# Gathering the next position's tokens ahead of the last turning of h in an expert stage

## The chip, the core and the metric

The kernel runs on one core of a Trainium2 chip as a single launch. The time is the device time of that core in microseconds (us), the median of several runs. The profile is one further execution of the same program, recorded by the hardware profiler. TensorE (PE) multiplies matrices, its weight loads are shown as PEld, VectorE is DVE, ScalarE is ACT, GpSimd is POOL, and SyncE (SP) issues the DMAs. Each engine runs its own list of instructions, and semaphores tie the lists together.

## What is computed

A two-layer encoder over 256 tokens of width 1024: a gated convolution and pooling mixer, cross-attention and a dense SwiGLU in the first layer; a Conformer convolution, cross-attention and a mixture of experts in the second; then an RMSNorm. The change is in the mixture of experts:

```python
def moe_swiglu(xn, router, w_gu, w_down):
    logits = (xn @ router).astype(jnp.float32)
    top_v, top_i = lax.top_k(logits, TOP_K)          # 2 of 8 experts for each token
    w = jax.nn.softmax(top_v, axis=-1)
    comb = jnp.sum(jax.nn.one_hot(top_i, N_EXPERTS, dtype=jnp.float32) * w[..., None],
                   axis=-2).astype(xn.dtype)
    out = jnp.zeros_like(xn)
    for e in range(N_EXPERTS):
        out = out + comb[..., e:e + 1] * swiglu(xn, w_gu[e], w_down[e])
    return out
```

with `swiglu(x) = (silu(x @ g) * (x @ u)) @ w_down`, g and u of 1024 x 3584 and w_down of 3584 x 1024 for each of the eight experts, all in float32.

## The kernel before

The experts are processed one after the other in eight "positions". For a position the tokens that chose its expert are gathered into `xg` by a product with a one-hot matrix, go through gate, up and down products, and their result is scattered back by a product with the turned one-hot matrix. Positions 2, 4 and 6 take experts with few tokens (at most 64, `NARROW`), positions 1, 3, 5 and 7 those with up to 128 (`WIDE`). So each narrow position is followed by a wide one.

A float32 operand is used as two parts: a rounded `hi`, made by a cast on ScalarE (L168), and the rest `lo`, made by a subtraction on VectorE (L169). Each weight chunk of 1 MB is loaded by one DMA, 13 chunks ahead, and is split in two halves into four buffers each for `hi` and for `lo`. A wide position multiplies the token parts separately, with three products for a pair. A narrow position lays the hi and lo parts of its 64 tokens side by side in 128 columns of `xg` (L1054, L1055), so that each weight part needs one product; the two halves of the result are added afterwards (`fold`, L1143).

A position has seven steps j. A step of a narrow position (`step_narrow`, L1163) makes the gate product `pg` and the up product `pu` of 512 hidden columns: `xs[:4]`, the first 512 columns of `xg`, in a first pass and `xs[4:]` in a second. The second pass of the up product takes its weights whole, without a split (L1193). In between it turns the h of the step before (L1155, `ht`, against a matrix that also adds the two halves), and it ends with that step's down products into `py`. h itself (`eh`, L1206) comes from the fold, a Silu on ScalarE and a multiplication on VectorE. After the seventh step three things are left: turning h of step 6 (`to_rows`, L1209, with the copy and the subtraction of L1054 and L1055 behind it), gathering the tokens of the following position (`following.rows`, L1069; for a wide one 16 products of 128 x 128 from L1043, `gx`, in two halves, each followed by a copy to the hi part, L1075, and a subtraction to the lo part, L1076, of `xg`), and the last down products. There is one `xg`.

The order on TensorE, VectorE and ScalarE in this stage is set by a scheduler that takes the program and places each instruction as soon as its inputs, its buffers and its engine are expected to be free. `tc.issue_after(i)` holds what is written inside it behind instruction i. Only the order on the queue that issues DMAs is as written.

Of the kernel before, what the change touches and what calls it, by code (L numbers as in the profile page):

```python
# [32 lines left out]
P = 128  # L33
D = 1024
# [41 lines left out]
def build(tc, io, cap=CAP):  # L76
    ctx = ExitStack()
    with ctx:
        _build(ctx, tc, io, cap)


def _build(ctx, tc, io, cap):
# [15 lines left out]
    V, S, G, PE = nc.vector, nc.scalar, nc.gpsimd, nc.tensor  # L98

    def f32(ap):  # L100
        return ap.bitcast(F32)

    def big_tile(name, dt=F32):
        return big.tile([P, CH], dt, tag="big", name=name)
# [7 lines left out]
    def tr_tile(name="tr", dt=F32):  # L112
        return psT.tile([P, 512], dt, tag="tr", name=name)
# [14 lines left out]
    def col(name, i=0):  # L128
        o = _OFF[name] + i
        return vec[:, o:o + 1]  # L130
# [19 lines left out]
    done, casts = [], []  # L150
# [553 lines left out]
    for m in range(KD):  # L704
# [6 lines left out]
        for hf in range(2):  # L711
# [4 lines left out]
            for kk in range(half):  # L716
                k = hf * half + kk
                h, sl = hid[k // 8], slice((k % 8) * T, (k % 8 + 1) * T)
# [22 lines left out]
    for k in range(KD):  # L741
        last = V.scalar_tensor_tensor(a3[:, k * T:(k + 1) * T], hT[:, k, :], col("od_norm_mix", k), rb,
                               op0=ALU.mult, op1=ALU.mult)
# [25 lines left out]
    def conv31(c):  # L769
        def tap(k):  # L770
            return glu[c][:, k:k + T], col("od_dw_w", c * CK + k)
        part = work.tile([P, T], F32, tag=("part", "sqs")[c % 2], name="part")
        src, w = tap(0)
        S.activation(part, src, AF.Identity, bias=col("od_dw_b", c), scale=w)
        taps = G_TAPS[c]
        for k in range(1, taps):
            src, w = tap(k)
            prod = work.tile([P, T], F32, tag="w1", name="prod", bufs=w1b)
            S.activation(prod, src, AF.Copy, scale=w)
            G.tensor_add(part, part, prod)  # L780
        y = tr_tile("cacc")[:, :T]
        src, w = tap(taps)
        V.tensor_scalar_mul(y, src, w)
        for k in range(taps + 1, CK):
            src, w = tap(k)
            V.scalar_tensor_tensor(y, src, w, y, op0=ALU.mult, op1=ALU.add)
        return V.tensor_add(cv[:, c * T:(c + 1) * T], y, part)
# [11 lines left out]
    last = conv31(KD - 1)  # L799
# [47 lines left out]
    for k in range(KD):  # L847
# [5 lines left out]
        last = V.tensor_sub(p2[1][:, sl], x1, f32(p2[0][:, sl]))  # L853
# [33 lines left out]
    xt = big_tile("xt")  # L887
# [149 lines left out]
    def gathered(oh, q):  # L1037

        px = tr_tile("gx")
        for kk in range(4):  # L1040
            d0 = (4 * q + kk) * P
            for t in range(2):
                PE.matmul(px[:, kk * P:(kk + 1) * P], xt[:, t * D + d0:t * D + d0 + P],  # L1043
                          oh[:, t, :], start=t == 0, stop=t == 1)
        return px

    def slots(p):
# [9 lines left out]
    class Gather:  # L1057
# [11 lines left out]
        def rows(self):  # L1069
            if self.e in NARROW:  # L1070
                return self.rows_narrow()
            for q in range(2):
                px = gathered(self.oh, q)
                hi, lo = xg[:, q * 512:(q + 1) * 512], xg[:, D + q * 512:D + (q + 1) * 512]
                S.copy(hi, px)  # L1075
                V.tensor_sub(lo, px, f32(hi))  # L1076

        def rows_narrow(self):
            px = tr_tile("gx")
            for k in range(KD):  # L1080
                for t in range(2):
                    PE.matmul(px[:, k * HALF:(k + 1) * HALF],
                              xt[:, t * D + k * P:t * D + (k + 1) * P],
                              self.oh[:, t, :HALF], start=t == 0, stop=t == 1)
            side_by_side(xg[:, :D], px)
# [42 lines left out]
    def expert(e, g, following):  # L1128
        nonlocal fn
        py = out_tiles()  # L1130
        two = e in NARROW

        def gate_up(j, gu):
            pz = acc_tile("gu")
            for kh in range(2):
                w = chunk()
                ws = [w(kk * 512, (kk + 1) * 512) for kk in range(4)]
                moving(pz, [(xg[:, k * P:(k + 1) * P], xg[:, D + k * P:D + (k + 1) * P])
                            for k in range(kh * 4, kh * 4 + 4)],
                       ws, kh == 0, kh == 1)  # L1140
            return pz
# [9 lines left out]
        def turn_narrow(j, h):  # L1151

            pt = tr_tile("ht")
            for i in range(4):
                ins = PE.matmul(pt[:, i * HALF:(i + 1) * HALF], h[:, i * P:(i + 1) * P], both,  # L1155
                                start=True, stop=True)
            return pt, ins

        def rows_narrow(j, pt):
            o = (j % 2) * D  # L1160
            side_by_side(ht[:, o:o + 512], pt[:, :4 * HALF])

        def step_narrow(j, h):  # L1163

            xs = [xg[:, k * P:(k + 1) * P] for k in range(KD)]
            tiles = [(f * 512, (f + 1) * 512) for f in range(4)]  # L1170

            def parts(w):
                return [w(*sl) for sl in tiles]
            pg, pu = acc_tile("gu"), acc_tile("gu")
            g0 = chunk()
            g1 = chunk()
            last = narrow(pg, xs[:4], parts(g0), True, False)
            u0 = chunk()
            if j:
                with tc.issue_after(last.ins):  # L1180
                    pt, last = turn_narrow(j - 1, h)
                with tc.issue_after(casts[-1].ins):
                    rows_narrow(j - 1, pt)
            with tc.issue_after(last.ins):
                narrow(pg, xs[4:], parts(g1), False, True)
            u1 = whole_chunk()
            d0 = chunk() if j else None
            narrow(pu, xs[:4], parts(u0), True, False)
            d1 = chunk() if j else None
            with tc.issue_after(casts[-2 if j else -1].ins):  # L1190
                sg = fold(pg)
            for kk in range(4):
                last = PE.matmul(pu, f32(xs[4 + kk]), u1[:, kk * 512:(kk + 1) * 512],  # L1193
                                 start=False, stop=kk == 3)
            with tc.issue_after(casts[-1].ins):
                h = gate(sg, pu)
            if j:
                down(j - 1, 0, d0)
                down(j - 1, 1, d1)
            return h  # L1200

        def gate(pg, pu):
            sg = pg if two else work.tile([P, 512], F32, tag="w2", name="esg", bufs=w2b)
            S.activation(sg, pg, AF.Silu, scale=g.cw[:, 1:2])
            h = work.tile([P, 512], F32, tag="w2", name="eh", bufs=w2b)
            V.scalar_tensor_tensor(h, pu, g.cw[:, 1:2], sg, op0=ALU.mult, op1=ALU.mult)  # L1206
            return h

        def to_rows(j, h):  # L1209
            pt = tr_tile("ht")  # L1210
            o = (j % 2) * D
            if two:
                return rows_narrow(j, turn_narrow(j, h)[0])
            for i in range(4):
                PE.transpose(pt[:, i * P:(i + 1) * P], h[:, i * P:(i + 1) * P], ident)
            S.copy(ht[:, o:o + 512], pt)
            V.tensor_sub(ht[:, o + 512:o + D], pt, f32(ht[:, o:o + 512]))
# [29 lines left out]
        h = None  # L1247
        for j in range(7):
            if two:
                h = step_narrow(j, h)  # L1250
                if j == 6:
                    to_rows(6, h)
                if following is not None and j in (3, 5):
                    following.step(j)
                continue
            pg = gate_up(j, 0)
            if j:
                to_rows(j - 1, h)
            pu = gate_up(j, 1)
            h = gate(pg, pu)  # L1260
            if j:
                down(j - 1, 0)
                if j == 6:
                    to_rows(6, h)
                down(j - 1, 1)
            if following is not None and j in (3, 5):
                following.step(j)
        if following is not None:
            following.rows()
        else:  # L1270
            fn = big_tile("fn")
            nc.sync.dma_start(fn[:, :D], io["final_norm"].to_broadcast([P, D]))
        down(6, 0)
        y = weighted(0)
        last = down(6, 1)
# [98 lines left out]
    for e in range(NE):  # L1374
        following = Gather(e + 1) if e + 1 < NE else None
# [7 lines left out]
    def overflow(e):  # L1383
        oh = one_hot(e, slots(e), P, F32)
        xo = big_tile("xo")
        for q in range(2):
            S.copy(xo[:, q * 512:(q + 1) * 512], gathered(oh, q))
# [164 lines left out]
```

## Time and profile before

| what | value |
|---|---|
| median of 3 runs (lowest, highest) | 1527.86 us (1527.21, 1529.25) |
| the profiled execution: its time / its span | 1527.87 us / 1526.1 us |
| TensorE busy | 1499.1 us, 98% of the span |
| VectorE, ScalarE, GpSimd busy | 85%, 69%, 10% |
| mean granted TensorE clock | 0.995 of full speed |
| read from HBM | 448.75 MB, 295 GB/s over the span |
| the expert stage | from about 587 us to about 1510 us |
| ends of positions 2, 4, 6 | about 931, 1157 and 1383 us |

Busy time of TensorE counts matmuls that follow each other through a pipeline, with modelled ends. In a row of the timeline the number in brackets is the time that the engine was idle before it, and behind the arrow what released it. One product of float32 operands shows as two records in the rows of `ht`, `gx` and the whole-weight pass (x8 for four products, x32 for sixteen).

### The profile page before, as it was taken

How to read it: one execution, taken by the hardware profiler on the slowest of the kernel's cores; microseconds unless marked ns; L12 is line 12 of the kernel's file. 1: busy time of each engine (PE TensorE's matmuls, PEld its weight loads, DVE VectorE, ACT ScalarE, POOL GpSimd, SP SyncE). 2: the span in 40 equal slices, each digit the busy share in tenths (PEclk: the TensorE clock that was granted, in tenths of full speed). 3: DMA queues.
4: the chain of work that ended last, by engine and by line, in shares of the span. 5: the costliest groups of instructions: out<-in, count | busy, mean ns of one | idle time of the engine just before them, and what ended most of it. 6: DMA issues, size and time to landing. Idle time of an engine off the chain costs nothing.

```text
span 1526.1 us, 23758 instructions
## 1 busy us (share of the span) xinstructions
PE 1499.1 (98%) x8558; PEld 1298.5 (85%) x8558; DVE 1302.1 (85%) x1735; ACT 1056.3 (69%) x1381; POOL 148.1 (10%) x230
## 2 busy tenths in 40 slices
PE   8999999999999999999999999999999999999996
PEld 8899999999988998888888777888777888777885
DVE  7876677776898867999898999998999998998996
ACT  6554554455576656777777887777887777887775
POOL 4710000001295201000000000000000000000000
PEclk9999999999999999999999999999999999999998
DMA  9754354426644665999999999999999999999940
GB/s 370 278 193 166 138 177 166 140 89 217 228 146 190 214 249 199 372 373 340 356 374 345 383 421 421 391 375 349 380 420 422 404 372 341 394 421 421 388 178 30
DMA packets 65215, 451.44 MB, mean 296 GB/s; under 512 B 7360, under 2 KB 7488, under 8 KB 12480
## 3 DMA queue, kind: packets, MB, share of 16 engines
q1 hardware_dynamic: 65088, 449.83, 76.9%
q8 instruction: 69, 1.13, 0.3%
q14 instruction: 58, 0.48, 0.1%
HBM read 448.75 MB, written 1.05 MB: 295 GB/s over the span
## 4 chain that ended last, share of the span: by engine, by line
PE 88%; POOL 4%; DVE 3%; ACT 2%; issue 1%; DMA 1%; SPq 0%; POOLq 0%; DVEq 0%; ACTq 0%
PE gu L217 8%; PE gu L213 8%; PE gu L212 8%; PE gu L1124 7%; PE acc L206 7%; PE acc L205 7%; PE acc L204 7%; PE py L1124 5%; PE gu L1193 4%; PE py L217 4%; PE py L212 4%; PE py L213 4%; POOL part L780 2%; PE ht L1155 1%; PE gx L1043 1%
## 5 line engine op out<-in xcount | busy, mean ns | idle before, releaser
L169 DVE TENSOR_TENSOR lo<-raw,hi 128x1024 fp32r<-128x1024 f32 (+3 forms) x573 | 673.2, 1209 | 101.1 <-ACT hi L168 81.3
L168 ACT CAST hi<-raw 128x1024 fp32r<-128x1024 f32 (+3 forms) x573 | 569.9, 1031 | 258.4 <-PE acc L205 89.7
L169 DVE TENSOR_TENSOR lo<-spare,hi 128x1024 fp32r<-128x1024 f32 (+1 forms) x226 | 261.7, 1201 | 17.5 <-ACT hi L168 12.1
L168 ACT CAST hi<-spare 128x1024 fp32r<-128x1024 f32 (+1 forms) x226 | 224.0, 1035 | 49.8 <-PE gu L213 27.9
L212 PE MATMUL gu<-hi,xg 128*128 128x512 f32 x560 | 219.5, 392 | 0.0
L213 PE MATMUL gu<-hi,xg 128*128 128x512 f32 x560 | 218.8, 391 | 0.0
L217 PE MATMUL gu<-lo,xg 128*128 128x512 f32 x560 | 157.3, 392 | 0.0
L212 PEld LDWEIGHTS gu<-hi,xg 128*128 128x128 f32 x560 | 105.2, 188 | 22.0 <-ACT hi L168 0.2
L213 PEld LDWEIGHTS gu<-hi,xg 128*128 128x128 f32 x560 | 105.3, 188 | 21.6
L217 PEld LDWEIGHTS gu<-lo,xg 128*128 128x128 f32 x560 | 104.8, 188 | 22.0
L212 PE MATMUL py<-hi,ht 128*128 128x512 f32 x280 | 109.4, 393 | 0.0
L213 PE MATMUL py<-hi,ht 128*128 128x512 f32 x280 | 109.3, 390 | 0.0
L206 PE MATMUL acc<-a2h,lo 128*128 128x256 f32 x336 | 95.4, 284 | 0.0
L205 PE MATMUL acc<-a2l,hi 128*128 128x256 f32 x336 | 95.3, 284 | 0.0
L204 PE MATMUL acc<-a2h,hi 128*128 128x256 f32 x336 | 95.3, 284 | 0.0
L1448 POOL TENSOR_TENSOR fo<-accum,fn 128x512 f32<-128x512 f32 x2 | 2.5, 1272 | 929.5 <-DVE accum L1245 929.5
L217 PE MATMUL py<-lo,ht 128*128 128x512 f32 x280 | 85.0, 396 | 0.0
L1124 PE MATMUL gu<-hi,xg 128*128 128x512 f32 x252 | 72.5, 401 | 0.0
L1124 PE MATMUL gu<-lo,xg 128*128 128x512 f32 x252 | 70.7, 392 | 0.0
L204 PEld LDWEIGHTS acc<-a2h,hi 128*128 128x128 f32 x336 | 64.6, 192 | 0.0
L205 PEld LDWEIGHTS acc<-a2l,hi 128*128 128x128 f32 x336 | 64.6, 192 | 0.0
L206 PEld LDWEIGHTS acc<-a2h,lo 128*128 128x128 f32 x336 | 64.6, 192 | 0.0
(424 smaller groups left out, 3144.1 us busy)
## 6 DMA issues: line engine op xcount, KB each, us to landing
raw<-in_moe_gu SPq DMA_DIRECT2D x139, 1024.0 KB, 7.2
spare<-in_moe_gu SPq DMA_DIRECT2D x85, 1024.0 KB, 7.7
raw<-in_moe_down SPq DMA_DIRECT2D x78, 1024.0 KB, 7.6
spare<-in_moe_down SPq DMA_DIRECT2D x32, 1024.0 KB, 7.5
raw<-in_ffn_gu SPq DMA_DIRECT2D x22, 1024.0 KB, 4.8
raw<-in_pw SPq DMA_DIRECT2D x12, 1024.0 KB, 4.8
raw<-in_ffn_down SPq DMA_DIRECT2D x16, 704.0 KB, 4.1
raw<-in_wk SPq DMA_DIRECT2D x8, 1024.0 KB, 7.2
```

The lines of the kernel that those rows point to most:

```text
L168: done[:] = (S.copy(hi[:, i:i + step], raw[:, a + i:a + i + step]), V.tensor_sub(lo[:, i:i + step], raw[:, a + i:a + i + step], f32(hi[:, ...
L169: V.tensor_sub(lo[:, i:i + step], raw[:, a + i:a + i + step], f32(hi[:, i:i + step])))
L204: PE.matmul(ps, a[0], b[0], start=first, stop=False)
L205: PE.matmul(ps, a[0], b[1], start=False, stop=False)
L206: PE.matmul(ps, a[1], b[0], start=False, stop=last)
L212: PE.matmul(ps, a[0], b[0], start=first and i == 0, stop=False)
L213: PE.matmul(ps, a[1], b[0], start=False, stop=False)
L217: ins = PE.matmul(ps, a[0], b[1], start=False, stop=last and i == n - 1)
L780: G.tensor_add(part, part, prod)
L1043: PE.matmul(px[:, kk * P:(kk + 1) * P], xt[:, t * D + d0:t * D + d0 + P], oh[:, t, :], start=t == 0, stop=t == 1)
L1124: ins = PE.matmul(ps, x, w[part], start=first and i == part == 0, stop=last and part == 1 and i == n - 1)
L1193: last = PE.matmul(pu, f32(xs[4 + kk]), u1[:, kk * 512:(kk + 1) * 512], start=False, stop=kk == 3)
```

## The change

The call of `to_rows(6, h)` of a narrow position moves from behind the last step to behind the gather for the following position, and it is held behind the gather's last product. For this, `gathered` notes its last product in `done`, and `rows` gives it back.

```diff
@@ gathered
             for t in range(2):
-                PE.matmul(px[:, kk * P:(kk + 1) * P], xt[:, t * D + d0:t * D + d0 + P],
-                          oh[:, t, :], start=t == 0, stop=t == 1)
+                done[:] = [PE.matmul(px[:, kk * P:(kk + 1) * P], xt[:, t * D + d0:t * D + d0 + P],
+                                     oh[:, t, :], start=t == 0, stop=t == 1)]
@@ Gather.rows
                 S.copy(hi, px)
                 V.tensor_sub(lo, px, f32(hi))
+            return done[0]
@@ expert
                 h = step_narrow(j, h)
-                if j == 6:
-                    to_rows(6, h)
                 if following is not None and j in (3, 5):
                     following.step(j)
                 continue
...
         if following is not None:
-            following.rows()
+            last = following.rows()
+            if two:
+
+                with tc.issue_after(last.ins):
+                    to_rows(6, h)
```

The products of the gather are not tied to anything in the last step, so the scheduler is free to place them inside it. On TensorE, at the end of position 2, from the turning of step 5's h inside step 6 (`gu` are the gate and up products, `py_9210` and `py_9211` the two halves of the down product), there stood before:

```order
L1155 MATMUL ht<-kept,eh 128x64 x4
L1124 MATMUL gu<-hi,xg 128x512 x4
L1124 MATMUL gu<-lo,xg 128x512 x4
L1124 MATMUL gu<-hi,xg 128x512 x4
L1124 MATMUL gu<-lo,xg 128x512 x4
L1193 MATMUL gu<-raw,xg 128x512 x4
L1124 MATMUL py_9210<-hi,ht 128x512 x4
L1124 MATMUL py_9210<-lo,ht 128x512 x4
L1124 MATMUL py_9211<-hi,ht 128x512 x4
L1124 MATMUL py_9211<-lo,ht 128x512 x4
L1155 MATMUL ht<-kept,eh 128x64 x4
L1043 MATMUL gx<-oh,xt 128x128 x16
```

Now, from two products further on:

```order
L1043 MATMUL gx<-oh,xt 128x128 x8
L1125 MATMUL gu<-hi,xg 128x512 x2
L1125 MATMUL gu<-lo,xg 128x512 x4
L1125 MATMUL gu<-hi,xg 128x512 x4
L1125 MATMUL gu<-lo,xg 128x512 x4
L1194 MATMUL gu<-raw,xg 128x512 x4
L1043 MATMUL gx<-oh,xt 128x128 x8
L1125 MATMUL py_9210<-hi,ht 128x512 x4
L1125 MATMUL py_9210<-lo,ht 128x512 x4
L1125 MATMUL py_9211<-hi,ht 128x512 x4
L1125 MATMUL py_9211<-lo,ht 128x512 x4
L1156 MATMUL ht<-kept,eh 128x64 x4
```

One half of the gather has moved into the gate product's second pass, the other behind the whole-weight pass. Directly behind the last row here stand the down products of step 6, as they stood behind the gather before.

On VectorE, from the subtraction that ends step 5's turning to the one that ends step 6's (`lo` are weight parts, `esg` the folded gate, `oh` the one-hot matrix of the position after the next), there stood before:

```order
L1055 TENSOR_TENSOR ht<-ht 128x4x64
L169 TENSOR_TENSOR lo<-raw,hi 128x1024 x4
L1148 TENSOR_TENSOR esg<-esg,gu 128x512
L169 TENSOR_TENSOR lo<-raw,hi 128x1024 x2
L1206 SCALAR_TENSOR_TENSOR eh<-gu,cw,esg 128x512
L169 TENSOR_TENSOR lo<-raw,hi 128x1024 x2
L1055 TENSOR_TENSOR ht<-ht 128x4x64
L1076 TENSOR_TENSOR xg<-gx,xg 128x512
L1031 TENSOR_SCALAR oh<-iota,placed 128x128 x2
L1076 TENSOR_TENSOR xg<-gx,xg 128x512
```

And now:

```order
L1055 TENSOR_TENSOR ht<-ht 128x4x64
L1076 TENSOR_TENSOR xg<-gx,xg 128x512
L169 TENSOR_TENSOR lo<-raw,hi 128x1024 x3
L1031 TENSOR_SCALAR oh<-iota,placed 128x128 x2
L169 TENSOR_TENSOR lo<-raw,hi 128x1024
L1149 TENSOR_TENSOR esg<-esg,gu 128x512
L1076 TENSOR_TENSOR xg<-gx,xg 128x512
L169 TENSOR_TENSOR lo<-raw,hi 128x1024 x2
L1207 SCALAR_TENSOR_TENSOR eh<-gu,cw,esg 128x512
L169 TENSOR_TENSOR lo<-raw,hi 128x1024 x2
L1055 TENSOR_TENSOR ht<-ht 128x4x64
```

The gather's two subtractions and the one-hot matrix stood behind h and its turning, and stand ahead of them now. On ScalarE it is the same: the first copy of the gather (L1075) now stands right behind the copy of step 5's turned rows, ahead of the four casts of step 5's down weights, and the second one behind the two copies of the fold, ahead of two more casts and the Silu. At the ends of positions 4 and 6 the three engines show the same pattern; at the last one there is no one-hot matrix, since no further position follows.

## Rows read from the trace of the kernel before

**Rows 1.** The chain of waits, share of the span by engine.

```profile
PE 88%; POOL 4%; DVE 3%; ACT 2%; issue 1%; DMA 1%; SPq 0%; POOLq 0%; DVEq 0%; ACTq 0%
```

**Rows 2.** TensorE's waits, 587 to 1526 us: total us, times, longest us.

```profile
PE ht L1155 <- DVE eh L1206: 3.0, 3, 1.0
PE so L1243 <- DVE yl L1235: 0.6, 1, 0.6
```

**Rows 3.** The DMA queue's waits, whole span: total us, times, longest us.

```profile
SPq L147 <- DVE lo L169: 804.5, 278, 14.0
```

**Rows 4.** Busy us by stretch: PE, PEld, DVE, ACT, POOL; clock, DMA share, GB/s.

```profile
830.00:931.00 101.00, 100.28 (x426) 74.10 (x425) 95.26 (x100) 83.56 (x101) 0.00 (x0) 1.00 0.98 394
931.00:1060.00 129.00, 128.62 (x619) 107.88 (x620) 116.66 (x116) 96.41 (x107) 0.00 (x0) 1.00 0.98 383
```

**Rows 5.** Timeline of TensorE, end of position 2: start us, us, instructions.

```profile
922.20 1.09 PE L1124 MATMUL gu<-lo,xg 128*128 128x512 f32 x4
...
926.16 1.49 PE L1124 MATMUL py<-hi,ht 128*128 128x512 f32 x4
...
928.41 1.08 PE L1124 MATMUL py<-hi,ht 128*128 128x512 f32 x4
929.33 1.07 PE L1124 MATMUL py<-lo,ht 128*128 128x512 f32 x4
931.38 1.11 PE L1155 MATMUL ht<-kept,eh 128*128 128x64 f32 x8 [0.98 <-DVE eh L1206]
932.32 3.79 PE L1043 MATMUL gx<-oh,xt 128*128 128x128 f32 x32
935.86 1.17 PE L1124 MATMUL py<-hi,ht 128*128 128x512 f32 x4
```

**Rows 6.** Timeline of ScalarE, end of position 2.

```profile
920.05 0.37 ACT L1054 CAST ht<-ht 128x256 fp32r<-128x256 f32 x1
920.32 3.90 ACT L168 CAST hi<-raw 128x1024 fp32r<-128x1024 f32 x4
924.24 0.58 ACT L1146 COPY esg<-gu 64x512 f32<-64x512 f32 x1
...
927.22 2.00 ACT L168 CAST hi<-raw 128x1024 fp32r<-128x1024 f32 x2 [1.81 <-PE py L1124]
929.12 0.72 ACT L1204 ACTIVATE esg<-esg,cw 128x512 f32<-128x512 f32 x1
...
934.36 0.58 ACT L1075 CAST xg<-gx 128x512 fp32r<-128x512 f32 x1 [1.47 <-PE gx L1043]
```

**Rows 7.** Timeline of VectorE, end of position 2.

```profile
922.64 4.62 DVE L169 TENSOR_TENSOR lo<-raw,hi 128x1024 fp32r<-128x1024 f32 x4
927.18 0.68 DVE L1148 TENSOR_TENSOR esg<-esg,gu 128x512 f32<-128x512 f32 x1
...
930.58 0.74 DVE L1206 SCALAR_TENSOR_TENSOR eh<-gu,cw,esg 128x512 f32<-128x512 f32 x1
931.24 2.35 DVE L169 TENSOR_TENSOR lo<-raw,hi 128x1024 fp32r<-128x1024 f32 x2
933.50 0.42 DVE L1055 TENSOR_TENSOR ht<-ht 128x256 fp32r<-128x256 f32 x1
...
936.15 0.61 DVE L1031 TENSOR_SCALAR oh<-iota,placed 128x128 f32<-128x128 f32 x2 [0.48 <-PE gx L1043]
936.76 0.69 DVE L1076 TENSOR_TENSOR xg<-gx,xg 128x512 fp32r<-128x512 f32 x1
```

**Rows 8.** Timeline of TensorE, the turnings at the ends of positions 4 and 6.

```profile
1157.04 1.10 PE L1155 MATMUL ht<-kept,eh 128*128 128x64 f32 x8 [1.00 <-DVE eh L1206]
...
1382.61 1.11 PE L1155 MATMUL ht<-kept,eh 128*128 128x64 f32 x8 [1.00 <-DVE eh L1206]
```

**Rows 9.** Timeline of TensorE, its one long idle time.

```profile
64.24 1.22 PE L613 MATMUL pool<-pm,ch 128*128 128x256 f32 x2 [3.58 <-POOL pm L608]
```

**Rows 10.** Busy us from there on, columns as in rows 4.

```profile
63.90:67.30 3.40, 3.06 (x12) 2.89 (x13) 3.40 (x9) 0.47 (x1) 0.33 (x2) 0.50 0.00 0
```

## The prediction

> **What bounds the kernel now.** I read the shares of the chain of waits first, then who waits for whom, then the three joins in the timeline. The chain is TensorE's to 88% [rows 1]. From the start of the expert stage on, TensorE's list of waits has two entries only: 3.0 us in three waits of the turning of h (`ht`, L1155) for `eh`, and one of 0.6 us [rows 2]. No weight is waited for there: it is the DMA queue that waits for buffers, 278 times for the `lo` subtraction that frees one [rows 3]. A wide position, between two narrow ones, keeps TensorE busy for 128.62 of 129.00 us [rows 4], so time lost at a join is not made good behind it. The change is therefore worth what it does to TensorE's stream at the three joins (end of positions 2, 4, 6), plus what it upsets elsewhere.
>
> **The join before.** TensorE's rows at the end of position 2 [rows 5]: the products of step 5 (`py`) stand from 926.16 and would let the engine go on at 929.33 + 0.92 = 930.25 (four of them go by in 0.92 us, as from 928.41 to 929.33). The turning starts at 931.38, since `eh` ends at 930.58 + 0.74 = 931.32 [rows 7]: a stall of 1.13 us, of which the row counts 0.98 as idle, since it models the ends of the products before. The turning lasts to 932.32 (0.94 us), the gather to 935.86 (3.54 us for 16 products), then the last step's products start. Behind the turning, VectorE subtracts the turned rows from 933.50 to 933.92 [rows 7]; the gather on TensorE hides this whole path. Joins two and three show the same wait, 1.00 us each [rows 8].
>
> **Part 1: where the gather goes.** In the order shown with the change, the 16 products are not simply swapped with the turning. Only the turning is tied to them; they themselves depend on nothing in step 6, and the scheduler puts 8 into the gate product's second half and 8 right behind the whole-weight pass. The amount of work is unchanged: 1.77 us twice. Everything behind the first half is 1.77 us later than before, everything from `py` on 3.54 us later. So without other effects TensorE would be free for the turning at 930.25 + 3.54 = 933.79.
>
> **Part 2: the copies that come with it.** The gather's result overwrites `xg`, of which there is one. The first copy (ScalarE, L1075) writes the columns that the up product's first pass still reads. That pass ended at 922.20 + 1.09 = 923.29 [rows 5], so now at 925.06. ScalarE runs its instructions in the order given, and the copy stands right behind the turned rows' copy that ends at 920.42 [rows 6]; ahead of it nothing is left to do. So ScalarE idles about 4.6 us, and behind the copy are queued the four casts of step 5's down weights, the two fold copies, the second gather copy, two more casts and the Silu. With the durations of [rows 6]: first copy to 925.64 (0.58), casts at 0.975 each (3.90 for four) to 926.62, 927.59, 928.57, 929.54, fold copies to 930.70, second copy to 931.29 (its gather is over at about 929.9), two casts to 933.29 (2.00), Silu to 934.01 (0.72). Of the fold copies, 0.58 each, one row stands for the two.
>
> VectorE's chain with the durations of [rows 7]: the copy's subtraction to 926.33; three `lo` at 1.155 (4.62 for four), the first when its cast is done, to 927.8, 928.9, 930.1; then the next one-hot matrix, 0.61, which waits for the gather's last product (it did before as well: [rows 7] shows that wait) and now stands ahead of h, to 930.7; the fourth `lo` to 931.9, the fold's sum (0.68) to 932.5, the second gather subtraction (0.69) to 933.2, two `lo` (2.35) to 935.6, `eh` (0.74) to 936.3. The Silu is ready by then, and so are the casts that `py` needs (the last `lo` at 931.9, needed near 932.9).
>
> So the turning starts at 936.38 and TensorE, free at 933.79, stalls 2.59 us instead of 1.13: **+1.46 us**. What fed the stall before was the chain of copies, not a lack of other work, and the gather's own copies now lengthen that chain.
>
> **Part 3: what stands behind the turning.** The last step's products need the turned rows with their subtraction, and the gather no longer lies between. VectorE has two `lo` queued ahead (936.32 to 938.67, from 2.35), then 0.42: 939.09. TensorE ends the turning at 936.38 + 0.94 = 937.32 and starts the products at 939.15: a new wait of **+1.83 us** on VectorE, where before there was none.
>
> **The sum.** 939.15 against 935.86: 3.29 us at a join. At the third there is no further position whose one-hot matrix is to be made, so 0.61 less: 2.68. Together 3.29 + 3.29 + 2.68 = 9.26 us. The profiled execution took 1527.87 us (span 1526.1), and the median of the runs is 1527.86, so the sum stands on the same base: 1537.1.
>
> **What is costed at nothing.** The same rearrangement moves some instructions of the wide positions by a few places (turnings and scatter products ahead of or behind four to eight gate products). Before, all of TensorE's waits in that stage outside the joins come to 0.6 us, so a gain is at most that; a turning moved ahead by four products, 0.9 us, could expose as much, at some five places: up to +4.5. I take 0, nearest to the row, since the products around them cover. The down weights of step 5 are cast about 5 us later and their buffers are refilled later by so much. A narrow position takes 2.4 us a chunk (101 us for 42 [rows 4]), 13 are fetched ahead, some 31 us, and the DMA queue waits for buffers and not the reverse [rows 3]; 5 us fit in. Nothing, then; if that cover were gone it could cost at most those 5 us once a join.
>
> **A rule against the change.** The trace has one long idle time of TensorE: 3.58 us before the pool product, and from there the granted clock is 0.50 for 3.40 us, 1.2 instead of 2.4 GHz, with full speed again behind [rows 9, 10]. At today's stalls of 1.13 us it stays at 1.00 [rows 4]. The Trainium skill, "TensorE: Matmul & The Clock Gate", section "HAM oscillation — how this bites in real kernels", says that waits between bursts of products bring the array back to its lower clock, and that each following burst then starts slow. The trace agrees at that one place. By the row, this costs half of 3.40, 1.7 us a join, 5.1 in all. The new stalls, 2.59 and 1.83 us with 0.94 of small products between, are each shorter than 3.58, and no row here shows which side they fall on; so it is a rival and not a term.
>
> **Rivals.**
> (a) The clock falls at the joins: 1537.1 + 5.1 = 1542.2; at one or two of them, between. For it: the new idle times lie close together. Against it: each is shorter than the only one that did it.
> (b) The stall on `eh` does not grow, because ScalarE or VectorE gets through its queue sooner than added up (the last casts overlap, the one-hot is no obstacle). Then only the uncovered subtraction is left. By the rows of before it ends 933.92 - 931.38 = 2.54 behind the turning's start, less 0.94 and with the same 0.06 to the next engine: 1.66 a join, 5.0 in all, 1532.9. For it: before, too, the stall followed `py` by a fixed chain. Against it: two copies, two subtractions and a one-hot matrix stand in the chain ahead of `eh` now.
> (c) Faster: the 3.54 us of gather fill the wait for `eh`, and the turned rows are ready when wanted. That saves 1.13 x 3 = 3.4 us: 1524.5. It is decided at one place: `eh` must end by 933.79, 2.5 us earlier than I have it, and the subtraction must come ahead of the two `lo`, which the order denies.
> (d) No change: the gain of (c) and the cost of part 3 cancel, 1527.9; this needs `eh` in time and the turned rows late by just the old stall.
>
> **Chances.** My forecast 0.72, with a range of its own of 1535 to 1539.5; (a) 0.12, (b) 0.10, (c) 0.03, (d) 0.03. The costs put at nothing widen it by a little on both sides. The range of 8 in 10 reaches down to the upper part of (b) at 1533.5 and up to the clock falling at two joins, 1541. About 0.2% (3 us) is what a measurement of this kernel can tell from no change. Faster 0.03, same 0.03, slower 0.94.
>
> **What would show it.** In the changed profile: TensorE's gather rows in two halves, ahead of the whole-weight pass's end and behind it; ScalarE idle some 4 to 5 us before the first gather copy, its releaser a gate or up product; TensorE idle 2 to 3 us before the turning of each narrow position's last step, released by `eh`, and then 1.5 to 2 us before the first `py` product behind it, released by the turned rows' subtraction; the third join some 0.6 us shorter than the others; clock 1.00 throughout. I am wrong if the turning's wait is near 1 us or gone, if the products behind it start without a wait, or if the expert stage has lost time between the joins.

## The result and the profile after

The changed kernel takes 1542.41 us (median of 4 runs, 1541.71 to 1543.62) where the kernel before takes 1528.51 (4 runs, 1527.21 to 1529.25): a ratio of 1.0092, 95% interval 1.008 to 1.0104. It is slower, as forecast, but by 13.9 us where 9.3 were forecast, and outside the range of 1533.5 to 1541.0. The profiled execution took 1543.07 us (span 1541.4), 15.20 more than that of before.

TensorE's waits from 587 us on, in total, times and longest, beside [rows 2]:

```profile
PE ht L1156 <- DVE eh L1207: 6.5, 3, 2.4
PE py L1125 <- DVE ht L1055: 4.3, 3, 1.4
PE so L1244 <- DVE yl L1236: 0.6, 1, 0.6
```

The wait for `eh` has grown from 3.0 to 6.5 us, and a wait of the last down products for the turned rows is new, 4.3. Together they are 7.8 us more, half of the 15.2. The timeline of TensorE at the end of position 2 shows the other half; its first row is the turning of step 5's h, its last the first product of the wide position. In the kernel before, these two rows are

```profile
918.54 1.00 PE L1155 MATMUL ht<-kept,eh 128*128 128x64 f32 x8
...
939.62 0.39 PE L212 MATMUL gu<-hi,xg 128*128 128x512 f32 x1
```

with [rows 5] between them, and now:

```profile
918.67 1.00 PE L1156 MATMUL ht<-kept,eh 128*128 128x64 f32 x8
...
928.43 1.95 PE L1043 MATMUL gx<-oh,xt 128*128 128x128 f32 x16
930.14 1.17 PE L1125 MATMUL py<-hi,ht 128*128 128x512 f32 x4
...
932.95 1.07 PE L1125 MATMUL py<-lo,ht 128*128 128x512 f32 x4
936.43 1.08 PE L1156 MATMUL ht<-kept,eh 128*128 128x64 f32 x8 [2.41 <-DVE eh L1207]
938.94 2.08 PE L1125 MATMUL py<-hi,ht 128*128 128x512 f32 x4 [1.43 <-DVE ht L1055]
940.81 1.91 PE L1125 MATMUL py<-lo,ht 128*128 128x512 f32 x4
942.52 1.91 PE L1125 MATMUL py<-hi,ht 128*128 128x512 f32 x4
944.23 1.37 PE L1125 MATMUL py<-lo,ht 128*128 128x512 f32 x4
945.44 0.40 PE L212 MATMUL gu<-hi,xg 128*128 128x512 f32 x1
```

Compare the four `py` groups behind the turning with the two shown ahead of it: a group of four that started some 0.92 us behind the last one, as in [rows 5], now starts 1.71 to 1.87 behind it. These products wait for nothing; they run slower. From 938.94 to 945.44 they take 6.50 us, and 3.76 in the kernel before (from 935.86 [rows 5] to 939.62 above). The granted clock says why. The columns are those of [rows 4]; the clock is the third number from the end:

```profile
923.00:936.40 13.40, 11.02 (x50) 7.77 (x49) 10.17 (x13) 10.51 (x13) 0.00 (x0) 1.00 1.01 422
936.40:938.30 1.90, 1.08 (x8) 0.97 (x8) 1.90 (x2) 0.37 (x1) 0.00 (x0) 0.93 1.02 423
938.30:945.20 6.90, 6.26 (x15) 4.94 (x16) 3.61 (x5) 4.27 (x5) 0.00 (x0) 0.52 1.01 416
945.20:952.00 6.80, 6.80 (x31) 5.56 (x30) 6.69 (x8) 4.85 (x6) 0.00 (x0) 1.00 1.02 422
946.00:1150.00 204.00, 204.00 (x911) 161.73 (x910) 189.09 (x188) 161.19 (x184) 0.00 (x0) 1.00 0.96 372
```

Through the first wait the clock stays up; during the second it falls to half, 1.2 GHz, and comes back just before the wide position begins. The last row is the wide position between two joins: busy 204.00 of 204.00 us, so nothing else is lost there.

ScalarE and VectorE in the same place, beside [rows 6] and [rows 7]:

```profile
920.19 0.36 ACT L1054 CAST ht<-ht 128x256 fp32r<-128x256 f32 x1
925.20 0.59 ACT L1075 CAST xg<-gx 128x512 fp32r<-128x512 f32 x1 [4.65 <-PE gu L1125]
925.68 3.88 ACT L168 CAST hi<-raw 128x1024 fp32r<-128x1024 f32 x4
...
933.17 0.72 ACT L1205 ACTIVATE esg<-esg,cw 128x512 f32<-128x512 f32 x1
```

```profile
926.76 3.50 DVE L169 TENSOR_TENSOR lo<-raw,hi 128x1024 fp32r<-128x1024 f32 x3 [0.25 <-ACT hi L168]
930.42 0.60 DVE L1031 TENSOR_SCALAR oh<-iota,placed 128x128 f32<-128x128 f32 x2 [0.16 <-PE gx L1043]
...
935.54 0.74 DVE L1207 SCALAR_TENSOR_TENSOR eh<-gu,cw,esg 128x512 f32<-128x512 f32 x1
936.20 2.35 DVE L169 TENSOR_TENSOR lo<-raw,hi 128x1024 fp32r<-128x1024 f32 x2
938.47 0.42 DVE L1055 TENSOR_TENSOR ht<-ht 128x256 fp32r<-128x256 f32 x1
```

The copy that waits 4.65 us for the up product, the casts queued behind it, the one-hot matrix ahead of h and the two `lo` ahead of the turned rows' subtraction are all where the prediction put them. At the other two joins [rows 8]:

```profile
1167.83 1.08 PE L1156 MATMUL ht<-kept,eh 128*128 128x64 f32 x8 [2.41 <-DVE eh L1207]
1170.34 2.08 PE L1125 MATMUL py<-hi,ht 128*128 128x512 f32 x4 [1.44 <-DVE ht L1055]
...
1397.15 1.08 PE L1156 MATMUL ht<-kept,eh 128*128 128x64 f32 x8 [1.65 <-DVE eh L1207]
1399.66 2.08 PE L1125 MATMUL py<-hi,ht 128*128 128x512 f32 x4 [1.43 <-DVE ht L1055]
```

### The profile page after: what moved, and what is told of

It reads as the page before. It is cut to its first block, busy times and chain, and to the rows that moved or that the text cites. A ratio compares the mean times of both kernels' runs of the same rounds, so it can differ in the third digit from the quotient of the medians.

```text
span 1541.4 us, 23747 instructions
## 1 busy us (share of the span) xinstructions
PE 1506.1 (98%) x8558; PEld 1302.9 (85%) x8558; DVE 1302.3 (84%) x1735; ACT 1057.7 (69%) x1381; POOL 148.2 (10%) x230
## 5 line engine op out<-in xcount | busy, mean ns | idle before, releaser
L169 DVE TENSOR_TENSOR lo<-spare,hi 128x1024 fp32r<-128x1024 f32 (+1 forms) x226 | 262.0, 1202 | 21.9 <-ACT hi L168 13.9
```

The costliest lines, as they stand in the source:

```text
L169: V.tensor_sub(lo[:, i:i + step], raw[:, a + i:a + i + step], f32(hi[:, i:i + step])))
```

## The experiments

**How they are read.** A whole run carries some scatter from the start: in the profiled executions the row that is 918.67 above stands between 918.2 and 920.5, with nothing changed ahead of it. So beside the median I give the length of each join, from the start of step 5's turning to the start of the wide position's first product (945.44 - 918.67 = 26.77 above), what TensorE idled in it (ahead of the turning + behind it), and for how long the clock stood at half. That is summed over slices of half a microsecond around the join: twice what the slice's granted clock lacks to 1, times its length. Each join is read from one profiled execution. A ratio is to the runs of the kernel before that were made beside that kernel (medians from 1528.09 to 1528.51 us).

| kernel | median us | ratio, 95% interval | joins 1, 2, 3: length, us | idle, us | half clock, us |
|---|---|---|---|---|---|
| before | 1528.51 | | 21.08, 21.08, 21.06 | 1.0, 1.0, 1.0 | 0, 0, 0 |
| changed | 1542.41 | 1.0092 (1.008, 1.0104) | 26.77, 25.54, 26.06 | 2.4+1.4, 2.4+1.4, 1.6+1.4 | 6.8, 3.4, 6.8 |
| fill_both | 1536.82 | 1.0057 (1.004, 1.0074) | 24.03, 24.05, 23.31 | 0.7+0.5, 0.7+0.5, 0.5 | 0, 0, 0 |
| fill_first | 1538.97 | 1.0069 (1.0053, 1.0086) | 25.63, 24.04, 23.26 | 0.7+1.4, 0.7+1.4, 1.4 | 3.4, 0, 0 |
| fill_second | 1538.05 | 1.0062 (1.0045, 1.0079) | 25.11, 24.91, 23.30 | 2.4, 2.4, 1.6+0.5 | 3.4, 3.4, 0 |
| late_oh | 1537.49 | 1.0059 (1.0042, 1.0076) | 23.30, 23.30, 23.27 | 0.5, 0.5, 0.5 | 0, 0, 0 |
| raw_behind | 1539.84 | 1.0072 (1.0057, 1.0088) | 26.10, 25.10, 23.99 | 1.2+2.0, 1.2+2.0, 2.0 | 6.8, 3.4, 3.4 |
| pinned | 1538.10 | 1.0063 (1.0048, 1.0078) | 26.56, 25.27, 21.49 | 2.5+0.9, 2.5+0.9, 0.3+0.9 | 6.8, 3.4, 0 |
| pinned_free | 1529.71 | 1.001 (1.0, 1.0019) | 20.93, 20.95, 20.92 | 0.9, 0.9, 0.9 | 0, 0, 0 |
| dose | 1544.41 | 1.01 (1.0084, 1.0115) | 25.95, 26.24, 24.65 | 2.9, 2.9, 2.9 | 6.8, 6.8, 3.4 |
| dose_one | 1530.59 | 1.0015 (1.0006, 1.0025) | 21.53, 21.54, 21.54 | 1.5, 1.5, 1.5 | 0, 0, 0 |
| silu_first | 1530.46 | 1.0014 (1.0004, 1.0024) | 21.65, 21.61, 21.62 | 1.6, 1.6, 1.6 | 0, 0, 0 |
| silu_first2 | 1524.90 | 0.9977 (0.9968, 0.9986) | 19.76, 19.77, 19.77 | 0, 0, 0 | 0, 0, 0 |

**Theory.** The loss has two parts: the order of the copies round the moved gather (the prediction's), and TensorE's clock, which falls because of the idle time that this order leaves. The rivals: one of the two alone; or the exchange of the two steps itself.

**fill_both** fills both idle times with products of 128x512 whose result nothing reads, two ahead of the turning and one behind it (each shows as two records).

```diff
+        def fill(behind, n):
+            with tc.issue_after(behind.ins):
+                ps = acc_tile("fill")
+                for _ in range(n):
+                    ins = PE.matmul(ps, xt[:, :P], xt[:, :512], start=True, stop=True)
+            return ins
...
+                last = fill(tail[0], 2)
                 with tc.issue_after(last.ins):
-                    to_rows(6, h)
+                    pt, turned_ = turn_narrow(6, h)
+                fill(turned_, 1)
+                rows_narrow(6, pt)
```

> The changed kernel with products of no use put into both idle times of each join: two of 128 x 512 (float32, about 0.86 us each) between the products of step 5 and the turning of step 6's h, and one between that turning and the last down products. Theory A (the idle times let the clock fall, and 7.0 of the 15.2 us between the two profiles are paid in the down products behind them at half clock): clock 1.00 at all three joins, the 16 down products behind the turning in 3.7 to 3.8 us instead of 5.3 to 6.6, time 1535 to 1537.5. Theory B (these products are slow for another reason, such as late casts or a busy memory): products as slow as in the changed kernel, time 1541 to 1544.

TensorE behind step 5's products, join 1:

```profile
934.00 1.88 PE L1254 MATMUL fill<-xt 128*128 128x512 f32 x4
936.57 1.08 PE L1156 MATMUL ht<-kept,eh 128*128 128x64 f32 x8 [0.69 <-DVE eh L1207]
...
939.08 1.20 PE L1125 MATMUL py<-hi,ht 128*128 128x512 f32 x4 [0.52 <-DVE ht L1055]
...
942.85 0.39 PE L212 MATMUL gu<-hi,xg 128*128 128x512 f32 x1
```

The turning and the products behind it start when they started in the changed kernel (17.75 and 20.26 us behind step 5's turning, where it has 17.76 and 20.27), but the products run at full clock: 3.77 us instead of 6.50. The joins are 2.95, 2.97 and 2.25 us longer than before, 8.17 in all: that is the order alone. The changed kernel's joins are another 2.74, 1.49 and 2.75 longer, 6.98: that is the clock. Theory A holds. By the medians the two parts are 8.6 and 5.3 us, which suggests that the clock's part differs from one execution to the next.

**fill_first and fill_second** fill one of the two idle times each. Against fill_both, fill_first leaves out the second product group and fill_second the first:

```diff
-                fill(turned_, 1)
```

```diff
-                last = fill(tail[0], 2)
```

> As with both idle times filled, but only the one ahead of the turning (2.4 us in the changed kernel); the 1.43 us behind the turning stay idle. Theory A1 (one idle time of 2.4 us is what lowers the clock): clock 1.00, 1535 to 1537.5. Theory A2 (what counts is how little the engine did over the two idle times together): with 0.7 + 1.4 us idle it should stay at 1.00 as well, since the joins of before did with one of 1.0. Theory A3 (the second idle time is enough by itself): clock 0.50 behind it, 1540 to 1544.

> As with both idle times filled, but only the one behind the turning; the 2.4 us ahead of it stay idle. Theory A1 (the one idle time of 2.4 us is enough): the clock falls at the joins as in the changed kernel, 1540 to 1544. Theory A2 (both together are needed): clock 1.00, 1535 to 1537.5.

The last down products' first row at joins 1 and 2 of fill_first, and the turning at join 1 of fill_second:

```profile
940.11 1.86 PE L1125 MATMUL py<-hi,ht 128*128 128x512 f32 x4 [1.44 <-DVE ht L1055]
...
1170.36 1.20 PE L1125 MATMUL py<-hi,ht 128*128 128x512 f32 x4 [1.44 <-DVE ht L1055]
```

```profile
936.55 1.08 PE L1156 MATMUL ht<-kept,eh 128*128 128x64 f32 x8 [2.41 <-DVE eh L1207]
```

With the idle time ahead of the turning filled, the clock fell at one join of three. Joins 1 and 2 have the same waits, 0.7 and 1.44, and only at the first did it fall. With the one behind the turning filled, it fell at both joins where the wait ahead is 2.41, so that one is enough by itself. Join 3 points to the two adding up: neither 1.65 ahead (with 0.52 behind) nor 1.44 behind alone brought the clock down there, and 1.65 and 1.43 together did, in the changed kernel. Each of the three is a single execution. Where the clock fell in these two kernels it stood at half for 3.4 us, where the changed kernel has 6.8 at two joins. Of what was expected, none of the three theories of fill_first holds at every join. A1 of fill_second is right on the clock at joins 1 and 2 and wrong on the time, 1538.05 for 1540 to 1544; A2 is wrong on the clock. The times of single runs, 1536.7 to 1541.0 for fill_first, spread more than those of fill_both, 1536.7 to 1537.0. That fits a clock that falls in some executions and not in others, but only one execution has a trace.

**late_oh** is fill_both with the one-hot matrix held behind the turned rows' subtraction.

```diff
-            if j == 3:
+            if j == 3 and held:
+                with tc.issue_after(held[0].ins):
+                    self.oh = one_hot(self.e, 0, slots(self.e), F32)
+            elif j == 3:
                 self.oh = one_hot(self.e, 0, slots(self.e), F32)
...
-                rows_narrow(6, pt)
+                held[:] = [rows_narrow(6, pt)]
```

> fill_both, with the one-hot of the position after next held on VectorE behind the turned rows' subtraction of the previous narrow position, so that it no longer stands ahead of h at joins 1 and 2. The prediction gave it 0.61 us of the turning's delay at each of these two joins, and nothing at join 3. Theory: h ends 0.6 us earlier at joins 1 and 2, 1.2 us in all: 1535.6 us against 1536.8 of fill_both, and the wait of 0.69 ahead of the turning goes at join 1. Rival (the one-hot filled time in which VectorE would have waited for ScalarE's casts): h ends when it did, 1536.8.

Joins 1 and 2 are 0.73 and 0.75 us shorter than in fill_both, join 3 is not (0.04): the matrix did delay h, at the two joins that have one. The median, 1537.49, does not show it, and is met by neither expectation. Its profiled execution reached join 1 1.67 us later than that of fill_both, and the two wide positions take 205.0 us each instead of 204.6, as they do in pinned_free, the other kernel that holds the matrix back.

**raw_behind** holds the whole gather behind the last whole-weight product, which takes the gather's first half out of the gate product and with it the copy at the head of ScalarE's queue.

```diff
+            tail[:] = [last]
...
-            last = following.rows()
             if two:
-
+                with tc.issue_after(tail[0].ins):
+                    last = following.rows()
```

> As the changed kernel, but the whole gather is held behind the last whole-weight product of step 6, so its first half no longer stands in the gate's second pass and ScalarE no longer stands idle 4.65 us behind a copy that waits for the up product. One-hot, gather subtractions and the turned rows' subtraction stay in VectorE's queue about where the changed kernel has them. Theory A1 (the copy at the head of ScalarE's queue makes most of the stall): h ends near 932.4 by rows 5 to 7 (931.2 of before, plus 0.6 for the one-hot and 0.6 for a gather subtraction ahead of it), while the down products of step 5 end at 933.9, so the turning does not wait; the last down products start within 1 us of where they stood: 1528.5 to 1531.5, clock 1.00. Theory A2 (the one-hot's wait for the gather's end makes the stall, wherever the first half stands): the turning still waits about 2 us, 1534 to 1541.

Neither of its two theories held; that 1539.84 lies in the range of A2 is luck, since the turning does not wait 2 us. ScalarE's first copy now waits 3.13 us, but behind the casts and the fold, and the turning's wait is halved, 1.19 at joins 1 and 2 and none at join 3. The copy's row at join 1:

```profile
928.34 0.59 ACT L1075 CAST xg<-gx 128x512 fp32r<-128x512 f32 x1 [3.13 <-PE gx L1043]
```

The wait behind the turning grew to 2.0 instead, and the clock fell at all three joins. Join 3, with that one wait alone, shows it in TensorE's rows:

```profile
1394.21 1.08 PE L1156 MATMUL ht<-kept,eh 128*128 128x64 f32 x8
1397.32 1.79 PE L1125 MATMUL py<-hi,ht 128*128 128x512 f32 x4 [2.03 <-DVE ht L1055]
1398.91 1.91 PE L1125 MATMUL py<-lo,ht 128*128 128x512 f32 x4
```

**pinned** holds the whole gather behind step 5's down products, so that it stands right ahead of the turning and nothing is hoisted.

```diff
-                down(j - 1, 1, d1)
+                tail[:] = [down(j - 1, 1, d1)]
...
-            last = following.rows()
             if two:
-
+                with tc.issue_after(tail[0].ins):
+                    last = following.rows()
```

> The exchange of the two steps is kept, but the whole gather is held behind the last product of step 5's down pass, so that none of it is hoisted into step 6 and no copy of it stands ahead of the casts and of Silu. Theory A (the cost of the changed kernel comes from where the scheduler puts the gather's halves, their copies and the one-hot, not from the exchange itself): h is ready as early as before, the turning stands behind 32 gather products and waits for nothing; what is left is the turned rows' subtraction, which on VectorE stands behind the one-hot and both gather subtractions. By rows 5 to 7 of before the gather would end near 933.7, the one-hot 934.3, one weight subtraction 935.5, two gather subtractions 936.8, the turned rows 937.2, so the last down products start near 937.4 instead of 935.9: 1.5 us at joins 1 and 2, some 0.8 at join 3 (no one-hot there), 3.8 in all, 1532.1 us; the wait behind the turning is then about 2.7 us, and where it lowers the clock 1.4 to 2.8 us come on top, up to 1537. Rival (the exchange itself costs, wherever the gather stands): 1536 to 1542, with a wait of about 2.4 us ahead of the turning. Rival (the subtraction's place costs nothing): 1528.

A miss for theory A: h is ready in time (`eh` ends at 931.60), and yet the turning waits. The last row is VectorE's.

```profile
930.51 3.73 PE L1043 MATMUL gx<-oh,xt 128*128 128x128 f32 x32
936.77 1.07 PE L1156 MATMUL ht<-kept,eh 128*128 128x64 f32 x8 [2.52 <-DVE xg L1076]
938.76 2.07 PE L1125 MATMUL py<-hi,ht 128*128 128x512 f32 x4 [0.92 <-DVE ht L1055]
...
935.94 1.28 DVE L1076 TENSOR_TENSOR xg<-gx,xg 128x512 fp32r<-128x512 f32 x2
```

The releaser is the gather's subtraction: the turning writes to a pool of two PSUM buffers (`tr_tile`), and the two halves of the gather hold both until VectorE has subtracted them, which it does behind the one-hot matrix. I had counted engines and not buffers. The first rival's time and wait came out, 1538.10 and 2.52 us, but not for its reason: the next kernel keeps the exchange and has no such wait.

**pinned_free** takes away what was found to cost, and leaves the exchange: the gather as in pinned, its halves in another PSUM pool of four buffers, its copies and the one-hot matrix behind the turned rows.

```diff
-                    last = following.rows()
-                with tc.issue_after(last.ins):
-                    to_rows(6, h)
+                    px = [gathered(following.oh, q, acc_tile) for q in range(2)]
+                with tc.issue_after(done[0].ins):
+                    turned = to_rows(6, h)
+                held[:] = [turned[1]]
+                with tc.issue_after(turned[0].ins), tc.issue_after(turned[1].ins):
+                    for q in range(2):
+                        following.kept(q, px[q])
```

> The exchange of the two steps alone, with the three things round it that cost taken away: the gather stands whole behind step 5's down products (as in pinned), its two halves go to buffers of the other PSUM pool, so that the turning does not wait for the first half's subtraction, and the gather's copies and subtractions and the one-hot stand behind the turned rows' copy and subtraction. By rows 5 to 7 of before: down products to 930.4, gather to 934.0, the turning right behind it to 934.9, its copy 935.4, its subtraction 935.8, the last down products 935.9 as before. Theory (the exchange in itself costs nothing, and saves nothing, since one wait of 1.0 us ahead of the turning turns into one of 1.0 us behind it): 1527.5 to 1529.5, clock as before. Rival (the exchange costs by itself, through the order of TensorE's work or the clock): 1533 or more.

```profile
931.40 3.73 PE L1043 MATMUL gx<-oh,xt 128*128 128x128 f32 x32
934.96 1.00 PE L1161 MATMUL ht<-kept,eh 128*128 128x64 f32 x8
936.89 1.20 PE L1130 MATMUL py<-hi,ht 128*128 128x512 f32 x4 [0.92 <-DVE ht L1055]
```

The joins are as long as before (0.15, 0.13 and 0.14 us shorter), with one wait of 0.92 behind the turning for one of 0.98 ahead of it. The two wide positions are 0.5 us longer each, and the whole is at most 0.2% slower. So the exchange in itself costs nothing at the joins, and brings nothing there. Pool, copies and matrix were changed together here; what each of them is worth alone is shown only for the matrix, by late_oh.

**dose** keeps the order of before and delays h: two products of the Silu's result with 1.0.

```diff
             S.activation(sg, pg, AF.Silu, scale=g.cw[:, 1:2])
+            if two and late:
+                for _ in range(2):
+                    V.tensor_single_scalar(sg, sg, 1.0, op=ALU.mult)
```

> The kernel before, its order kept, with two products of a 128x512 tile with 1.0 put on VectorE between Silu and h at the end of each narrow position (h unchanged by them): it measures what a longer stall ahead of the turning costs in the old order, without the exchange. Each takes 0.35 to 0.7 us, so the turning waits 1.7 to 2.4 us instead of 1.0 and the gather and the last down products follow without a second wait. Theory (a single wait costs its own length, and the clock stays, since 32 gather products and 16 down products follow at once): 3 times 0.7 to 1.4, 1530.4 to 1532.5, clock 1.00. Rival (a wait of that length lowers the clock as in fill_second): 1.4 to 2.8 us more at each join where it falls, 1533 to 1540.

The scheduler let a third `lo` ahead of h as well, so the wait is 2.93 us. The clock fell at all three joins, here in the turning and the gather, which follow at once. TensorE's rows, and the columns of [rows 4] for the stretch behind the wait:

```profile
934.85 1.97 PE L1155 MATMUL ht<-kept,eh 128*128 128x64 f32 x8 [2.93 <-DVE eh L1209]
936.61 5.93 PE L1043 MATMUL gx<-oh,xt 128*128 128x128 f32 x32
```

```profile
934.80:938.20 3.40, 3.35 (x15) 3.35 (x16) 1.56 (x2) 0.37 (x1) 0.00 (x0) 0.50 1.00 414
```

The rival's mechanism is right: one longer wait in the old order, with 3.54 us of gather work behind it, is enough, and without any exchange this kernel is about as slow as the changed one. Its 1544.41 us lie above the rival's 1533 to 1540, since the wait is longer than planned and the clock fell at every join.

**dose_one** has one such product instead of two.

```diff
-                for _ in range(2):
+                for _ in range(1):
```

> As dose, with one product of a 128x512 tile with 1.0 between Silu and h instead of two (0.44 us each there), and no weight subtraction slips ahead of h beside it: the turning waits 1.4 us instead of 1.0, once a join, in the old order. Theory (the clock stays at waits of this length and falls at 2.4 to 2.9): 3 times 0.44, 1529.7 us beside 1528.4, clock as before, turning at 1.00. Rival (any lengthening of this wait brings the clock down, as the 1.4 us of fill_first did at one join of three): up to 3.4 us more at each join where it falls, 1531 to 1538.

The theory holds at the joins: the wait is 1.49, the clock stays at 1.00 at all three, and each is 0.45 to 0.48 us longer. A wait of this length costs itself and no more. The median is 2.5 us above the runs beside it, 1.4 of it in the joins; its profiled execution reached join 1 1.3 us late.

**silu_first** goes back to the order of before and takes its own stall away: the last down pass's first weights are cast and subtracted behind Silu and h, at the end of a narrow position.

```diff
+            gated[:] = [silu, V.scalar_tensor_tensor(h, pu, g.cw[:, 1:2], sg, op0=ALU.mult, op1=ALU.mult)]
...
-        down(6, 0)
+        if two:
+            with tc.issue_after(gated[0].ins), tc.issue_after(gated[1].ins):
+                w6 = chunk()
+        down(6, 0, w6)
```

> The kernel before, with one thing held: at a narrow position's end the casts and subtractions of the last down product's first weights stand behind the Silu and behind h, and not ahead of them. Theory C (at the joins h is late because ScalarE and VectorE have two casts and two subtractions queued ahead of it, not because its inputs are late): h ends about 929.4 on the old time scale instead of 931.32, ahead of the end of step 5's products at 930.25, the stall of 1.13 us is gone at all three joins, the gather still covers the turned rows: 1524 to 1526 against 1528.5. Theory D (h waits for its inputs or the casts are needed sooner): 1527.5 to 1530, with the stall kept or moved to the last down products.

A miss for theory C, and slower than before: the turning no longer waits, but now four `lo` stand between h and the turned rows' subtraction, and the gather's second half waits for the PSUM buffer that this subtraction frees:

```profile
935.62 2.05 PE L1043 MATMUL gx<-oh,xt 128*128 128x128 f32 x16 [1.59 <-DVE ht L1055]
```

**silu_first2** also holds the last pass's second weights, behind the turned rows' copy and subtraction.

```diff
+                    turned = to_rows(6, h)
...
+        w7 = None
+        if two:
+            with tc.issue_after(turned[0].ins), tc.issue_after(turned[1].ins):
+                w7 = chunk()
-        last = down(6, 1)
+        last = down(6, 1, w7)
```

> The kernel before with the order of its two steps kept. Of the two weight chunks of the last down pass at a narrow position's end, the first is cast and subtracted behind Silu and h (as in silu_first), the second behind the turned rows' copy and subtraction. Theory: both waits go, the 1.0 us ahead of the turning and the 1.6 us ahead of the gather's second half that silu_first put in its place, and nothing new waits: 0.98 us a join, 2.9 in all, 1525.4 us beside 1528.3 (ratio 0.998). Rival: the last down products now wait for their weights, whose subtractions end later: 1528 or more, with a wait of py behind lo. Rival: the time of step 6 is set by the weights' arrival and not by TensorE, and the gain is given back in the wide position: no change.

```profile
928.98 1.07 PE L1124 MATMUL py<-lo,ht 128*128 128x512 f32 x4
929.89 1.00 PE L1155 MATMUL ht<-kept,eh 128*128 128x64 f32 x8
930.72 3.79 PE L1043 MATMUL gx<-oh,xt 128*128 128x128 f32 x32
934.27 1.17 PE L1124 MATMUL py<-hi,ht 128*128 128x512 f32 x4
```

No wait is left at the joins; each is 1.3 us shorter, 3.9 in all. At 1524.90 us (11 runs, 1524.38 to 1525.83) this is faster than both kernels, by 0.1 to 0.3% than the kernel before.

## Why the prediction was wrong

The step that failed is the one under "A rule against the change": the new stalls "are each shorter than 3.58, and no row here shows which side they fall on; so it is a rival and not a term". It should have been a term. fill_both gives its size: 6.98 us of the 15.2 between the two profiled executions. The one reason held against it, that each stall is shorter than the only idle time that had lowered the clock, was none, for that row says nothing of shorter ones: dose shows that 2.93 us does it at every join, fill_second that 2.41 does, and raw_behind that 2.03 can. And the stalls were weighed one by one, where join 3 of fill_first, fill_second and the changed kernel points to two near ones bringing the clock down together that did not do it alone. A chance of 0.12 for rival (a) was far too low, and the range took in the clock at two joins, not at three. Of the signs that the prediction named, "clock 1.00 throughout" failed at all three joins. The Trainium skill, "TensorE: Matmul & The Clock Gate", section "HAM oscillation — how this bites in real kernels", tells of a kernel whose waits of some 3 to 5 us between bursts of products brought the clock down, so that the next burst started slow; it was right to weigh. This trace agrees in kind, 0.52 of full speed behind waits of 2.41 and 1.43 us, but here shorter waits did it, and the measurement decides.

- The size of the clock's term: 1.7 us a join was taken from [rows 10]; it was 2.74, 1.49 and 2.75, since at two joins the half clock lasted twice as long. That rival (a)'s 1542.2 comes so close to 1542.41 is luck: its term for the clock is too small by 1.9 us in the profiled execution, and its term for the order, the next point, too large by 1.2.
- The order's term, 9.26: measured 8.10 in the changed kernel up to the first `py` (2.95, 2.95 and 2.20), and 8.17 in fill_both. The stall ahead of the turning was right (2.59 forecast; 936.43 less 932.95 + 0.92 is 2.56). The wait behind it was 1.57 (938.94 less 936.43 + 0.94) where 1.83 were forecast: an instruction on VectorE starts some 0.08 us before the one ahead of it ends (936.20, where 935.54 + 0.74 is 936.28), and a sum of durations counts that twice. At join 3 the missing one-hot matrix gave 0.75 and not 0.61; late_oh measures the same at joins 1 and 2.
- Part 1 and part 2 hold row by row: both halves of the gather, ScalarE's idle time (4.65 for about 4.6), the one-hot matrix behind the gather's end, `eh` at 936.28 for 936.3 (936.15 if the 0.13 us by which this execution reached the join later are taken off).
- Rival (b), that the stall on `eh` does not grow, is out: 6.5 us for 3.0. Rivals (c) and (d) needed h early; pinned_free shows that the exchange brings nothing at the joins even then, since the turned rows' path of copy and subtraction, which the gather hid before, comes out in its place.
- What was costed at nothing cost nothing: the wide position between joins 1 and 2 lasts 204.63 us from its first product to the next join, 204.58 before.

## What to carry to other kernels

Where TensorE is the bound and its clock can fall, price a new wait twice: its own length, and the work behind it at half clock, and add up waits that lie close together before asking whether they are short. When a block of work is moved, follow its copies through the queues of the other engines, and the buffers that it holds; here the order of those copies cost 8.17 us at the joins, and the exchange of the products none. And before moving work to cover a wait, see which instructions stand ahead of the awaited one in its queue: here holding two chunks of casts back did what moving the gather was meant for.

## What the runs showed of the hardware

That waits well below 3.58 us lower TensorE's clock was not expected. Over the 39 joins of the table, each in one execution: where TensorE idled 1.6 us or less in all, the clock never fell (23 joins); between 2.0 and 2.2 it fell at two of four; from 2.4 on at all 12. It stood at half for 3.4 us at eight joins and for 6.8 at six. What decides between these two, and why joins with the same waits differ, these runs don't tell.
